# A transformer encoder on one core: the mixers' pieces in another order, with other loads at the start and another final norm

## The chip, the cores and the metric

The kernel runs on one core of one Trainium2 chip. A core has five engines with a program each: TensorE (PE in the profile; PEld is its loading of weights), VectorE (DVE), ScalarE (ACT), GpSimd (POOL) and SyncE (SP), which here only issues DMAs. Each engine works through its own instructions strictly in their order and waits on semaphores of the others. The metric is device time in microseconds of one execution. The kernel before takes 1120.86 us (median of 3 runs, 1120.8 to 1122.6).

## The reference

The input is one sequence of 256 tokens with 1024 channels, all float32. There are two layers, each with two half-weighted feed-forward parts around a mixer:

```python
for l in range(DEPTH):
    x = x + 0.5 * swiglu(rms_norm(x, ln_ffn1[l]), ffn1_w_in[l], ffn1_w_out[l])
    h = rms_norm(x, ln_mix[l])
    x = x + hybrid_mixer(h, w_mix_in[l], conv_w[l], ..., w_mix_out[l], lam_init)
    x = x + 0.5 * swiglu(rms_norm(x, ln_ffn2[l]), ffn2_w_in[l], ffn2_w_out[l])
return rms_norm(x, ln_final)
```

The mixer projects h once and splits it into three kinds of heads, whose outputs are put side by side and projected back:

```python
(wq, wk, wv, dq, dk, dv, dn_qkv, dn_z, dn_beta, dn_a) = jnp.split(h @ w_in, cuts, axis=-1)
o_win = window_attention(wq, wk, wv, sink, slopes)          # 6 query heads on 2 key heads
o_d = diff_attention(dq, dk, dv, lam, slopes)               # 4 heads, difference of two softmaxes
o_diff = rms_norm(o_d, diff_g) * (1.0 - lam_init)
q, k, v = jnp.split(silu(short_conv(dn_qkv, conv_w)), ...)  # 6 heads, width-5 convolution
o_c = gated_delta_chunked(q, k, v, beta, g) + (the same, backwards in time)
o_dn = rms_norm(o_c, dn_g) * silu(dn_z)
return concatenate([o_win, o_diff, o_dn]) @ w_out
```

`gated_delta_chunked` works in 4 chunks of 64 tokens. In each chunk and head, in both directions, it solves a triangular system of 64 (the chunk inverses below, 48 of them), and then a scan carries a 64 x 64 state over the chunks.

## The kernel before, in words

Activations lie transposed in SBUF: `x` is 128 partitions x 8 blocks of channels (`KD`) x 256 tokens.

**Feed-forward.** Weights come from HBM through SP's DMAs in tiles of 128x1024 (512 KB), into 8 raw buffers `wr`. Each is split into two parts of reduced precision: ACT rounds it (`wh`, L264) and DVE takes the residual (`wl`, L265). Each block of 128x256 then takes three matmuls, activation high x weight high, low x high, high x low (`mm3`, L270 to L272). The first two tiles are loaded and split in four parts each (`start`, `ar`, `ah`, `al`, L101 and L102), together with x in four parts, so that the first matmuls can begin early; `prep` scales x by the norm's gain (`xh`, L243, `xl`, L244), and the norm's reciprocal is applied behind the matmuls, so that they needn't wait for it. `sq_add` squares x (L194) and sums (L198); `norm_scale` sums over the channels with a matmul (`fin_ps` and the like, L211), takes a reciprocal root on 128x2 numbers and spreads it (L220).

**Mixer.** It is cut into pieces, and the table `ORDER` is the order in which the program issues them. A scheduler then places the instructions of each piece in each engine's program, and weights are loaded ahead in the order in which the pieces read them. The pieces of which the texts speak:

- `A:n` token projection (`pv`): values and gate inputs. `c:i:b` convolution: a projection (`pj`, L455, 8 matmuls of f32, which the trace counts as 16), taps on ACT and DVE (`pad`, L562, L568). `co` turns conv outputs to tokens (`ptr`), `qn` and `qc` norm q and k and bring them to channels (`kq`, L626).
- `G`, `GS`, `GE`, `GT`: gates, their running sums (`pg`, L507 and L508), exponentials and rows. `E:i` decay exponentials (`XE` from `pe`, L642). `X:p:h` their products with q·k (`pq`, L658).
- `ic`, `i`, `ir:a:b`, `im`, `io`, `ie`: the inverses. `i` transposes XE to `Dg` (L842) and then `L`; `ir` to `io` are a chain of products (`pr`, L825) and sums (`Vi` or `pp`, L826) on DVE, the io's merging blocks of the inverse to larger ones; `ie` transposes `Vi` to `Vc` and `Vt` (L930, L933), multiplies on PE with the gated inputs (`WA`, `W`, `Qc`, L939 to L965).
- `p:n`: projections of attention, 9 to 11 the three groups of local (window) queries, 12 the local keys (`wq`, L683), 13 to 16 the diff heads' queries and keys (`dqk`, L686). `w:b` local scores (L699) and their softmax (L710 to L723), `hw:b` local outputs; `d:h` diff scores (L732, L737, softmax L740 to L753), `h:n` their outputs (`pT`, `PT`, `pso`).
- `sa`, `sb`, `sc`: the scan's steps (`px`, `pS`, `pw`, `pk`, `po`, L995). `z:n` gate projection (`pz`, L466), `ze` its silu (`zt`, L977). `oT` transposes outputs (`pto`), `on` norms the scan's output, `o:part:d` the output projection (`py`).

Some small operations can be given to POOL (with ACT) in place of DVE; `SHARED` lists those that are. `BANK` says for each PSUM tile from which pool it comes: `pm` (2 buffers), `pd` (4), `pt` (2). `lt` loads ACT's table of logarithm and exponential (L202).

**Final norm.** When the last feed-forward has written x, `final` multiplies x with gain and norm in eight operations of 128x256 (`fo`, L1129) and writes it out in four DMAs.

Of the kernel before, what the change touches and what calls it, by code (L numbers as in the profile page):

```python
# [31 lines left out]
NROW = 158  # L32
C_U0, C_U1, C_ONE, C_ID, C_MM = 0, 128, 256, 384, 512
# [23 lines left out]
class Kernel:  # L57
    def __init__(self, ctx, tc, ins, out):
# [12 lines left out]
        self.x = self.xp.tile([P, KD, S], F32, tag="x", name="x")  # L71
        self.col = cp.tile([P, 150], F32, name="col")
# [3 lines left out]
        warm = cp.tile([P, 1], F32, name="warm")  # L76
        nc.scalar.activation(warm, self.onec, AF.Copy)

    def start(self, gcol, pool=None, src=None):

        nc = self.nc
        n = KD // 2
        self.ahead = []
        if pool is not None:
            for j in range(2):
                w, go = self.fetch(src, j * 1024, 1024, n, pool)
                h = pool.tile([P, 1024], F32R, name=f"ah{j}")
                lo = pool.tile([P, 1024], F32R, name=f"al{j}")
                self.ahead.append((w, go, h, lo))
        for i in range(n):  # L90
            nc.sync.dma_start(self.x[:, 2 * i : 2 * i + 2, :], self.ins["x"][:, 2 * i : 2 * i + 2, :])
            for w, go, h, lo in self.ahead:
                go[i]()
            if i == 0:
                nc.scalar.dma_start(self.col, self.ins["cols"])
        for i in range(n):
            for k in (2 * i, 2 * i + 1):
                self.prep(k, gcol, False)
            c = slice(i * 256, i * 256 + 256)
            for w, go, h, lo in self.ahead:  # L100
                nc.scalar.activation(h[:, c], w[:, c], AF.Copy)  # L101
                nc.vector.tensor_tensor(lo[:, c], w[:, c], h[:, c].bitcast(F32), ALU.subtract)  # L102
        self.ahead = [a[2:] for a in self.ahead]
# [99 lines left out]

    def norm_scale(self, name, last=False, log=True):

        nc = self.nc
        ps = self.psum([P, 512], f"{name}_ps", "pt")
        for p in range(2):
            parts = [t for t in (self.sq, self.sq7) if t is not None]
            for t in parts:  # L210
                nc.tensor.matmul(  # L211
                    ps[:, p : p + 1], lhsT=t[:, p * P : (p + 1) * P], rhs=self.onec, start=t is parts[0], stop=t is parts[-1]
                )
        v = self.sp.tile([P, 2], F32, tag="nv", name=f"{name}_v")
# [60 lines left out]
    def ffn(self, l, i, gnext, first, late=False):  # L275
# [3 lines left out]
        with tc.tile_pool(name=f"hp{nm}", bufs=1) as hp, tc.tile_pool(name=f"ht{nm}", bufs=3) as ht:  # L279
# [19 lines left out]
            for j in range(NF):  # L299
# [47 lines left out]
            for d in range(KD):  # L347
# [20 lines left out]
    def mixer(self, l, gnext):  # L368
# [22 lines left out]
        with ExitStack() as ctx:  # L391
# [676 lines left out]
            def out_proj(part, d):  # L1068
# [20 lines left out]
            pieces = {  # L1089
                "clear": clear, "lt": self.log_table, "N": norm, "V": values, "G": gates, "GS": gate_sums, "GE": gate_exps, "GT": gate_rows,  # L1090
# [197 lines left out]
```

## Time and profile before

| | |
|---|---|
| median of 3 runs | 1120.86 us (1120.8 to 1122.6) |
| the profiled execution | 1121.32 us |
| its span, first to last instruction | 1119.5 us |
| mean granted TensorE clock | 0.991 |
| start to the first matmul | 5.86 us |
| first mixer, first `pv` matmul to the output projection's end | 197.6 to about 374 us |
| second mixer | 746.9 to about 924 us |
| last feed-forward matmul begins | 1108.36 us |

The profile is of one execution. The page gives busy times, a chain followed back from the last instruction, and groups of instructions. A timeline lists the instructions in order of time: start, duration, engine, line, operation, output and inputs, form, count, and in brackets how long the engine had been idle and what ended that. Where several alike follow each other they are one row, with a count. The two mixers are alike, so one is read closely.

### The profile page before, as it was taken

What the parts mean: (1) busy time and instruction counts of PE and PEld (TensorE: products, weight loads), DVE (VectorE), ACT (ScalarE), POOL (GpSimd) and SP (SyncE); (2) the same over time, 40 slices, a digit from 0 to 9 for tenths busy, and PEclk for the clock granted to TensorE, in tenths of its full rate; (3) what the DMA queues carried; (4) which work ended last, traced back from release to release, by engine and by line L of the source; (5) the groups of instructions that cost most, each with busy time, mean ns of one, the idle gap of its engine ahead of it and who ended that gap; (6) DMA issues with size and microseconds to landing.
All of it is one profiled execution on the core that took longest, in us unless ns stands there. A gap on an engine that the chain in (4) does not pass through costs nothing.

```text
span 1119.5 us, 22207 instructions
## 1 busy us (share of the span) xinstructions
PE 1077.2 (96%) x9098; PEld 1009.7 (90%) x9098; DVE 751.0 (67%) x1374; ACT 545.4 (49%) x1006; POOL 60.1 (5%) x109
## 2 busy tenths in 40 slices
PE   7999999999799999999999999999989999999996
PEld 7999999777568999999999999988756789999996
DVE  7766654579958866666566666536897697666643
ACT  6544433263773654544444454423648455445441
POOL 0000001100101000000000000121010010000010
PEclk9999999999899999999999999999989999999998
DMA  9655654422322555565555565534223135555521
GB/s 331 225 182 187 199 178 136 132 94 95 113 96 77 165 174 189 182 200 184 171 174 184 188 197 182 170 115 150 85 85 132 42 130 172 189 183 195 187 95 38
DMA packets 49637, 173.65 MB, mean 155 GB/s; under 512 B 5504, under 2 KB 6784, under 8 KB 49536
## 3 DMA queue, kind: packets, MB, share of 16 engines
q1 hardware_dynamic: 49104, 171.64, 46.2%
q8 instruction: 71, 1.16, 0.4%
q10 hardware_dynamic: 432, 0.60, 0.2%
q14 instruction: 30, 0.25, 0.1%
HBM read 171.17 MB, written 1.05 MB: 154 GB/s over the span
## 4 chain that ended last, share of the span: by engine, by line
PE 78%; DVE 13%; ACT 4%; issue 3%; DMA 1%; POOL 1%; DVEq 0%; SPq 0%; ACTq 0%
PE ps L272 21%; PE ps L270 21%; PE ps L271 21%; PE pj L455 4%; PE pv L466 2%; DVE pr L825 2%; DVE wl L265 2%; PE py L270 1%; DVE pp L826 1%; PE py L271 1%; PE py L272 1%; DVE pad L568 1%; ACT wh L264 1%; DVE mxd L740 1%; PE px L995 1%
## 5 line engine op out<-in xcount | busy, mean ns | idle before, releaser
L265 DVE TENSOR_TENSOR wl<-wr,wh 128x1024 fp32r<-128x1024 f32 x270 | 330.5, 1226 | 167.6 <-ACT wh L264 167.1
L264 ACT ACTIVATE wh<-wr 128x1024 fp32r<-128x1024 f32 x270 | 284.2, 1054 | 243.9 <-issue 153.0
L270 PE MATMUL ps<-xh,wh 128*128 128x256 f32 x1336 | 378.6, 283 | 0.6 <-ACT wh L264 0.6
L272 PE MATMUL ps<-xh,wl 128*128 128x256 f32 x1336 | 378.3, 283 | 0.8 <-DVE wl L265 0.8
L271 PE MATMUL ps<-xl,wh 128*128 128x256 f32 x1336 | 377.9, 283 | 0.0
L272 PEld LDWEIGHTS ps<-xh,wl 128*128 128x128 f32 x1336 | 256.3, 192 | 1.2 <-DVE wl L265 1.2
L270 PEld LDWEIGHTS ps<-xh,wh 128*128 128x128 f32 x1336 | 256.3, 192 | 0.8 <-ACT wh L264 0.8
L271 PEld LDWEIGHTS ps<-xl,wh 128*128 128x128 f32 x1336 | 256.3, 192 | 0.0
L270 PE MATMUL ps<-hh,wh 128*128 128x256 f32 x672 | 190.2, 283 | 0.0
L271 PE MATMUL ps<-hl,wh 128*128 128x256 f32 x672 | 190.2, 283 | 0.0
L272 PE MATMUL ps<-hh,wl 128*128 128x256 f32 x672 | 190.2, 283 | 0.0
L455 PE MATMUL pj<-xf,wr 128*128 128x256 f32 x544 | 128.8, 387 | 1.2 <-DVE dqk L686 1.2
L270 PEld LDWEIGHTS ps<-hh,wh 128*128 128x128 f32 x672 | 129.0, 192 | 0.0
L271 PEld LDWEIGHTS ps<-hl,wh 128*128 128x128 f32 x672 | 129.0, 192 | 0.0
L272 PEld LDWEIGHTS ps<-hh,wl 128*128 128x128 f32 x672 | 129.0, 192 | 0.0
L455 PEld LDWEIGHTS pj<-xf,wr 128*128 128x128 f32 x544 | 101.7, 193 | 18.3 <-issue 3.9
L293 ACT ACTIVATE hh<-h 128x256 fp32r<-128x256 f32 x88 | 36.1, 416 | 90.3 <-DVE h L291 90.3
L198 POOL TENSOR_TENSOR sqacc<-sqacc,sqt 128x256 f32<-128x256 f32 x27 | 24.5, 907 | 741.6 <-ACT sqt L194 741.6
L288 DVE TENSOR_TENSOR t<-ps,f_rb 128x256 f32<-128x256 f32 x88 | 36.9, 424 | 38.0 <-PE ps L272 37.7
L294 DVE TENSOR_TENSOR hl<-h,hh 128x256 fp32r<-128x256 f32 x88 | 36.8, 423 | 30.4 <-ACT hh L293 30.4
L194 ACT ACTIVATE sqt<-x 128x256 f32<-128x256 f32 x49 | 19.8, 409 | 56.3 <-DVE x L361 52.5
L568 DVE SCALAR_TENSOR_TENSOR pad<-pad,cwh 128x256 f32<-128x256 f32 x68 | 33.1, 487 | 12.1 <-ACT pad L562 6.8
(319 smaller groups left out, 1212.7 us busy)
## 6 DMA issues: line engine op xcount, KB each, us to landing
wr<-in_ffn SPq DMA_DIRECT2D x258, 512.0 KB, 3.4
wr<-in_mix SPq DMA_DIRECT2D x50, 512.0 KB, 3.4
wr<-in_mix SPq DMA_DIRECT2D x8, 408.0 KB, 3.1
wr<-in_mix SPq DMA_DIRECT2D x8, 384.0 KB, 2.9
x<-in_x SPq DMA_DIRECT2D x4, 256.0 KB, 4.1
ar<-in_ffn SPq DMA_DIRECT2D x8, 128.0 KB, 4.2
cb<-in_constb SPq DMA_DIRECT2D x1, 588.0 KB, 10.2
out_y<-fo SPq DMA_DIRECT2D x2, 256.0 KB, 2.4
```

Of the source, the lines that this page charges most:

```text
L198: (eng or nc.gpsimd).tensor_tensor(self.sq, self.sq, t, ALU.add)
L264: nc.scalar.activation(h, w, AF.Copy)
L265: nc.vector.tensor_tensor(lo, w, h.bitcast(F32), ALU.subtract)
L270: mm(out, lhsT=ah, rhs=bh, start=start, stop=False)
L271: mm(out, lhsT=ah, rhs=bl, start=False, stop=False)
L272: mm(out, lhsT=al, rhs=bh, start=False, stop=stop)
L288: nc.vector.tensor_tensor(t[:rows], gate, rb[:rows], ALU.mult)
L293: nc.scalar.activation(hh[:n, j, :], h[:n], AF.Copy)
L294: nc.vector.tensor_tensor(hl[:n, j, :], h[:n], hh[:n, j, :].bitcast(F32), ALU.subtract)
L455: mm(ps[:, 0:S], lhsT=w[:, k * P : (k + 1) * P], rhs=xf[:, k, :], start=k == 0, stop=k == KD - 1)
L466: mm(st[name][p][:, 0:n], lhsT=xf[:, k, p * P : (p + 1) * P], rhs=w[:, c], start=k == 0, stop=k == KD - 1)
L568: stt(cv, pad[:, w : w + S], cw[:, i * 5 + w : i * 5 + w + 1], cv, ALU.mult, ALU.add)
```

## The change

1. `ORDER` is another order of nearly the same pieces (both layers use it). Behind the token projection the convolution's projections come ahead of the gates; local and diff projections, heads and scores interleave otherwise with the inverses' merges (`io`); the gate projection `z` begins around `ie`, where before it came last in the table; the scan's last step moves behind `on:1`. `BANK` moves the PSUM tiles pq, p1, po, pso and pto from `pd` (4 buffers) to `pt` (2). `SHARED` has 16 entries for 12.
2. At the start x and the table of gains are one DRAM tensor and one tile, loaded by three DMAs from ACT's queue (662, 512 and 1024 columns). The first two weight tiles are packed anew (channel blocks 0 to 3 of both halves in the first, 4 to 7 in the second) and loaded by three DMAs from SP in place of eight. Their split takes four operations of 128x512 on ACT and on DVE for eight of 128x256. Six matmuls on a zero tile are issued ahead of all others.
3. In the final norm ACT multiplies x with the gain (`xg`) while the last feed-forward's outputs are added, three matmuls with no use for their result are issued ahead of the sums and three behind them, and DVE's last multiplication is four operations of 128x512.

```diff
 ORDER = """
...
-io:0 p:9 d:1 p:12 io:1 d:3 w:0 h:2 h:1 p:10 io:2 io:3 io:4 h:3 p:11 w:1 w:2 h:0 hw:0 io:5 ie ce:2 dn hw:1 f g:0 hw:2
...
+io:0 d:3 co:2:2 h:2 p:9 io:1 d:0 w:0 io:2 io:3 h:3 p:10 h:1 p:11 w:1 w:2 io:4 h:0 io:5 hw:0 hw:1 ce:2 ie z:0 dn f z:1
...
 """
-SHARED = set("O2 d0 d1 d2 d3 g5 s3 t1 t8 x4 x5 x6".split())
+SHARED = set("O3 S1 d0 d1 d2 d3 g2 g5 s4 t0 t3 t8 x0 x4 x6 x7".split())
...
     def start(self, gcol, pool=None, src=None):
+            zero = pool.tile([P, S], F32, name="zero")
+            nc.vector.memset(zero, 0.0)
+            wm = self.psum([P, 512], "wm", "pt")
+            for i in range(NWARM):
+                nc.tensor.matmul(wm[:, 0:S], lhsT=zero[:, 0:P], rhs=zero, start=True, stop=True)
             for j in range(2):
-                w, go = self.fetch(src, j * 1024, 1024, n, pool)
+                w, g = self.fetch(src, j * 1024, 1024, 2 - j, pool)
+                go += g
-        for i in range(n):
-            nc.sync.dma_start(self.x[:, 2 * i : 2 * i + 2, :], self.ins["x"][:, 2 * i : 2 * i + 2, :])
-            for w, go, h, lo in self.ahead:
-                go[i]()
-            if i == 0:
-                nc.scalar.dma_start(self.col, self.ins["cols"])
+        cuts = [0] + [NCOL + 512 * i for i in (1, 2, 4)]
+        for a, b in zip(cuts, cuts[1:]):
+            nc.scalar.dma_start(self.xc[:, a:b], self.ins["x"][:, a:b])
...
+    def idle_mm(self, n, tag="pm"):
+        ps = self.psum([P, 512], "idle", tag)
+        for i in range(n):
+            self.nc.tensor.matmul(ps[:, 0:S], lhsT=self.ident, rhs=self.cst[:, C_U0 : C_U0 + S], start=True, stop=True)
...
                 if gnext is None:
                     self.sq_add(d, last=d == KD - 1)
+                    if d == 0:
+                        self.xg = self.xp.tile([P, KD, S], F32, tag="xh", name="xg")
+                    nc.scalar.activation(self.xg[:, d, :], self.x[:, d, :], AF.Copy, scale=self.col[:, 48 + d : 49 + d])
...
     def final(self, name):
-        for k in range(KD):
-            nc.vector.scalar_tensor_tensor(o[:, k, :], self.x[:, k, :], self.col[:, 48 + k : 49 + k], rb, ALU.mult, ALU.mult)
+        for i in range(KD // 2):
+            k = slice(2 * i, 2 * i + 2)
+            nc.vector.tensor_tensor(o[:, k, :], self.xg[:, k, :], rb.unsqueeze(1).to_broadcast([P, 2, S]), ALU.mult)
```

Three places in the first mixer show what the new table does to the engines' programs. Lines of the changed kernel have moved by 12 to 27.

On PE, behind the token projection (`pv`), the kernel before goes through five blocks of conv projections and then the gate sums (`pg`):

```order
L466 MATMUL pv<-wr,xf 128x408 x2
L455 MATMUL pj<-xf,wr 128x256 x40
L507 MATMUL pg<-bgs,cst 128x12 x2
L508 MATMUL pg<-bgs,cst 128x24
L436 MATMUL ptr<-cst,cs 128x128 x2
```

The changed kernel has there:

```order
L493 MATMUL pv<-wr,xf 128x408 x2
L482 MATMUL pj<-xf,wr 128x256 x40
L463 MATMUL ptr<-cst,cs 128x128 x4
L482 MATMUL pj<-xf,wr 128x256 x8
L463 MATMUL ptr<-cst,cs 128x128 x4
L482 MATMUL pj<-xf,wr 128x256 x8
L534 MATMUL pg<-bgs,cst 128x12 x2
L535 MATMUL pg<-bgs,cst 128x24
```

Two more blocks of projections and two groups of transposes now stand ahead of the gate sums.

On DVE, around the inverses' first merges, the kernel before has this ahead of the first local scores (`wq` comes first for the queries p:9, then for the keys p:12; `pr` is a product and `Vi` or `pp` a sum of the inverses, `mxd`, `smd` and `c` belong to the diff heads' softmax):

```order
L683 SCALAR_TENSOR_TENSOR wq<-pj,m_rb 128x256
L825 TENSOR_TENSOR pr<-L,Vi 128x1024
L747 RECIPROCAL c_3108<-smd 128x2
L740 TENSOR_REDUCE mxd<-pss 128x2
L748 SCALAR_TENSOR_TENSOR c_3108<-smd,nlam,c_3108 128x2
L740 TENSOR_REDUCE mxd<-pss 128x2
L749 RECIPROCAL smd<-smd 128x2
L826 TENSOR_REDUCE pp<-pr 128x16x8
L825 TENSOR_TENSOR pr<-Vi,pp 128x1024
L265 TENSOR_TENSOR wl<-wr,wh 128x1024
L747 RECIPROCAL c_3163<-smd 128x2
L683 SCALAR_TENSOR_TENSOR wq<-pj,m_rb 128x256
```

The changed kernel has this there (`wq` is now that of the keys):

```order
L710 SCALAR_TENSOR_TENSOR wq<-pj,m_rb 128x256
L853 TENSOR_REDUCE pp<-pr 128x8x8
L774 RECIPROCAL c_3112<-smd 128x2
L767 TENSOR_REDUCE mxd<-pss 128x2
L775 SCALAR_TENSOR_TENSOR c_3112<-smd,nlam,c_3112 128x2
L767 TENSOR_REDUCE mxd<-pss 128x2
L776 RECIPROCAL smd<-smd 128x2
L852 TENSOR_TENSOR pr<-L,Vi 128x1024
L853 TENSOR_REDUCE pp<-pr 128x16x8
L774 RECIPROCAL c_3151<-smd 128x2
L852 TENSOR_TENSOR pr<-Vi,pp 128x1024
L775 SCALAR_TENSOR_TENSOR c_3151<-smd,nlam,c_3151 128x2
```

The keys' `wq` has moved ahead by a merge's products; that of the queries comes next behind the last row, behind the product `pr` and with no weight residual (`wl`) between.

On PE the first local scores (`pss` from `wq`) stand so in the kernel before:

```order
L737 MATMUL pss<-dqk 128x256 x4
L699 MATMUL pss<-wq 128x256 x4
L455 MATMUL pj<-xf,wr 128x256 x4
L436 MATMUL pT<-cst,sc 128x128 x4
L455 MATMUL pj<-xf,wr 128x256 x4
```

In the changed kernel the first local scores have this ahead of them:

```order
L463 MATMUL pT<-cst,sc 128x128 x4
L482 MATMUL pj<-xf,wr 128x256 x8
L811 MATMUL pso<-V,PT 128x64 x4
L759 LDWEIGHTS sdiag
L759 MATMUL pss<-ddb,sdiag 128x512
L759 LDWEIGHTS sdiag
L759 MATMUL pss<-ddb,sdiag 128x512
L764 MATMUL pss<-dqk 128x256 x4
L726 MATMUL pss<-wq 128x256 x4
```

A diff head's output and another one's scores now stand ahead of them.

On ACT, at the inverses' end, the kernel before has (`W` and `WA` are copies of the inverses, `zt` the silu of the gate projection, `p` the products with them, `oh` attention outputs):

```order
L942 COPY W<-Vt 32x12x32 x2
L791 ACTIVATE hn<-O 128x512
L765 ACTIVATE PT<-pT 128x512 x2
L977 ACTIVATE zt<-pz,rth 128x384 x2
L775 ACTIVATE oh<-pso 128x256
L202 ACT_TABLE_LOAD
L956 ACTIVATE Qc<-p_3494 128x384
L765 ACTIVATE PT<-pT 128x512
L965 COPY W<-p_3544 32x12x32
L765 ACTIVATE PT<-pT 128x512
L965 COPY W<-p_3592 32x12x32
L775 ACTIVATE oh<-pso 128x256
```

The changed kernel has there:

```order
L969 COPY W<-Vt 32x12x32 x2
L802 ACTIVATE oh<-pso 128x256
L818 ACTIVATE hn<-O 128x512
L792 ACTIVATE PT<-pT 128x512
L983 ACTIVATE Qc<-p_3501 128x384
L792 ACTIVATE PT<-pT 128x512
L1004 ACTIVATE zt<-pz,rth 128x384
L992 COPY W<-p_3561 32x12x32
L992 COPY W<-p_3588 32x12x32
L1004 ACTIVATE zt<-pz,rth 128x384
L214 ACT_TABLE_LOAD
L1045 ACTIVATE SC<-px 128x384
```

Both `zt` and the table load have moved from ahead of `Qc` to behind it.

More of the change, by code (lines that the diff above doesn't have):

```diff
@@ L32 @@
 NROW = 158
+NCOL = 150
+NWARM = 6
 C_U0, C_U1, C_ONE, C_ID, C_MM = 0, 128, 256, 384, 512
@@ L47 @@
 BANK = dict(
-    pj="pm", pv="pd", pz="pm", py="pm", pss="pd", pg="pt", pgr="pd", ptr="pd", pkq="pt", pe="pd", pq="pd", p1="pd",
-    p2="pt", pk="pd", px="pt", pS="pt", po="pd", pw="pt", pT="pd", pso="pd", pto="pd",
+    pj="pm", pv="pd", pz="pm", py="pm", pss="pd", pg="pt", pgr="pd", ptr="pd", pkq="pt", pe="pd", pq="pt", p1="pt",
+    p2="pt", pk="pd", px="pt", pS="pt", po="pt", pw="pt", pT="pd", pso="pt", pto="pt",
 )
-SHARED = set("O2 d0 d1 d2 d3 g5 s3 t1 t8 x4 x5 x6".split())
+SHARED = set("O3 S1 d0 d1 d2 d3 g2 g5 s4 t0 t3 t8 x0 x4 x6 x7".split())
 C_M0, C_M1, C_DD, C_WD, C_SEL = 0, 64, 128, 640, 1152
@@ L70, in __init__ @@
         cp = self.cp
-        self.x = self.xp.tile([P, KD, S], F32, tag="x", name="x")
-        self.col = cp.tile([P, 150], F32, name="col")
+        self.xc = self.xp.tile([P, NCOL + KD * S], F32, tag="x", name="x")
+        self.col = self.xc[:, 0:NCOL]
+        self.x = self.xc[:, NCOL:].rearrange("p (k t) -> p k t", k=KD)
         self.cst = None
@@ L75, in __init__ @@
         nc.vector.memset(self.onec, 1.0)
-        warm = cp.tile([P, 1], F32, name="warm")
-        nc.scalar.activation(warm, self.onec, AF.Copy)
     def start(self, gcol, pool=None, src=None):
         nc = self.nc
+        self.ahead = []
         n = KD // 2
-        self.ahead = []
+        go = []
         if pool is not None:
+            zero = pool.tile([P, S], F32, name="zero")
[3 more added lines that the diff above has]
+                nc.tensor.matmul(wm[:, 0:S], lhsT=zero[:, 0:P], rhs=zero, start=True, stop=True)
             for j in range(2):
-                w, go = self.fetch(src, j * 1024, 1024, n, pool)
+                w, g = self.fetch(src, j * 1024, 1024, 2 - j, pool)
+                go += g
                 h = pool.tile([P, 1024], F32R, name=f"ah{j}")
                 lo = pool.tile([P, 1024], F32R, name=f"al{j}")
-                self.ahead.append((w, go, h, lo))
-        for i in range(n):
-            nc.sync.dma_start(self.x[:, 2 * i : 2 * i + 2, :], self.ins["x"][:, 2 * i : 2 * i + 2, :])
-            for w, go, h, lo in self.ahead:
-                go[i]()
-            if i == 0:
-                nc.scalar.dma_start(self.col, self.ins["cols"])
+                self.ahead.append((w, h, lo))
+        cuts = [0] + [NCOL + 512 * i for i in (1, 2, 4)]
+        for a, b in zip(cuts, cuts[1:]):
+            nc.scalar.dma_start(self.xc[:, a:b], self.ins["x"][:, a:b])
+        warm = self.cp.tile([P, 1], F32, name="warm")
+        nc.scalar.activation(warm, self.onec, AF.Copy)
+        for g in go:
+            g()
         for i in range(n):
@@ L98, in start @@
                 self.prep(k, gcol, False)
-            c = slice(i * 256, i * 256 + 256)
-            for w, go, h, lo in self.ahead:
+            if self.ahead:
+                w, h, lo = self.ahead[i // 2]
+                c = slice(i % 2 * 512, i % 2 * 512 + 512)
                 nc.scalar.activation(h[:, c], w[:, c], AF.Copy)
                 nc.vector.tensor_tensor(lo[:, c], w[:, c], h[:, c].bitcast(F32), ALU.subtract)
-        self.ahead = [a[2:] for a in self.ahead]
+        self.ahead = [a[1:] for a in self.ahead]
     def constants(self):
@@ L213, in norm_scale @@
                 )
+        if last:
+            self.idle_mm(3)
         v = self.sp.tile([P, 2], F32, tag="nv", name=f"{name}_v")
```

28 lines of the change are left out of this document (17 added, 11 removed).

## The prediction

> **What bounds the kernel now.** I read the page first, for the shares and the chain that ended last.
>
> ```profile
> span 1119.5 us, 22207 instructions
> PE 1077.2 (96%) x9098; PEld 1009.7 (90%) x9098; DVE 751.0 (67%) x1374; ACT 545.4 (49%) x1006; POOL 60.1 (5%) x109
> PE 78%; DVE 13%; ACT 4%; issue 3%; DMA 1%; POOL 1%; DVEq 0%; SPq 0%; ACTq 0%
> ```
>
> PE is busy for 1077.2 of 1119.5 us, so 42.3 us are all that any order can win on it. The chain leaves PE for 22% of the span, and mostly for DVE. That share is an average, so next comes the view by windows: the stretch, its length, then busy time and number of instructions of PE, PEld, DVE, ACT and POOL, the granted clock, the DMA share, GB/s.
>
> ```profile
> 14.00:197.00 183.00, 181.57 (x1508) 181.04 (x1509) 115.37 (x180) 83.78 (x116) 5.78 (x6) 1.00 0.59 200
> 230.00:250.00 20.00, 18.84 (x150) 15.04 (x148) 15.33 (x49) 17.27 (x58) 1.14 (x7) 1.00 0.24 79
> 250.00:285.00 35.00, 29.85 (x151) 23.04 (x148) 34.48 (x66) 14.12 (x38) 3.27 (x3) 0.98 0.29 91
> 285.00:300.00 15.00, 12.60 (x64) 10.15 (x64) 13.98 (x22) 9.00 (x22) 3.55 (x2) 0.82 0.45 141
> 300.00:315.00 15.00, 13.81 (x76) 8.89 (x75) 12.61 (x31) 14.82 (x46) 0.00 (x0) 1.00 0.32 114
> 330.00:345.00 15.00, 14.61 (x319) 13.28 (x314) 10.65 (x20) 4.14 (x9) 1.02 (x1) 1.00 0.01 2
> 345.00:360.00 15.00, 14.03 (x204) 13.14 (x201) 14.00 (x30) 6.43 (x14) 2.41 (x10) 1.00 0.33 106
> 835.00:850.00 15.00, 13.71 (x70) 10.99 (x70) 13.69 (x20) 9.79 (x25) 3.55 (x2) 0.84 0.41 141
> ```
>
> The feed-forward stages (first row) leave PE 1.4 us of idle in 183; the change does not touch their middle. What can move is in the two mixers, of which the rows show the first (197 to about 374) and, last, the slow place of the second (747 to about 924), which looks the same. Each mixer has three limits in turn. From 250 to 300 it is DVE, busy for 48.46 of 50 us, with the inverses of the chunk matrices. From 300 to 315 it is ACT, with the softmaxes. After 330 it is PE. The largest hole on PE lies under the DVE part, and the timeline there shows why (start, length, engine, line, operation, in brackets idle time and what ended it):
>
> ```profile
> 281.88 2.66 DVE L825 TENSOR_TENSOR pr<-Vi,pp 128x1024 f32<-128x1024 f32 x1
> 284.45 1.22 DVE L265 TENSOR_TENSOR wl<-wr,wh 128x1024 fp32r<-128x1024 f32 x1
> 285.66 0.41 DVE L683 SCALAR_TENSOR_TENSOR wq<-pj,m_rb 128x256 f32<-128x256 f32 x1
> 286.21 2.17 PE L699 MATMUL pss<-wq 64*128 64x256 f32 x8 [5.77 <-DVE c L748]
> 288.31 2.97 PE L455 MATMUL pj<-xf,wr 128*128 128x256 f32 x8
> ```
>
> PE stands for 5.77 us. The profile names c, the last small DVE operation; the one that PE needs is wq, the local key, which started behind a 2.66 us product and a weight residual. Afterwards eight projection matmuls cost 2.97 us, where the 80 of a row further down cost 17.43, or 1.74 for eight; the granted clock of that window is 0.82. So the hole costs PE 5.77 us and then some 15 x 0.18 = 2.7 us of clock, 12.6/15 of it in busy time: 2.3. **8.1 us per mixer** is what stands there to be had.
>
> **The change, part by part.**
>
> *Local projections earlier.* In the new order the keys' projection (p:12) comes a merge and more ahead of the local scores, and head 0's diff scores with the matmuls of head 2's output stand between. The wq that PE waited for is done well before; what PE waits for now is wq of the first query group, behind another such product on DVE, but with other work in front of it (16 projection matmuls of the trace's count at 0.22, 3.5 us, transposes, diff scores). I take the 5.77 us as gone from PE. It does not follow that the mixer is 5.77 us shorter: DVE is busy in 48.46 of 50 us there, and its work is not less. It issues the same products, reductions, residuals and scalings; one slope operation moves to PE, and one more piece (the late conv piece c:2:2, with its sums) comes in from before. I count +0.6 to +0.8 us of DVE work between the start of the inverses and their end. What DVE can win is its idle time there, 1.5 us. So the end of the inverses, Vc, moves by the sum of that and of its start.
>
> *Gate sums later.* This is the part that could hurt.
>
> ```profile
> 209.53 17.43 PE L455 MATMUL pj<-xf,wr 128*128 128x256 f32 x80
> 226.79 0.51 PE L507 MATMUL pg<-bgs,cst 128*128 128x12 f32 x4
> 231.09 0.69 PE L436 MATMUL ptr<-cst,cs 128*128 128x128 f32 x4
> 236.42 1.38 ACT L642 ACTIVATE XE<-pe,ngc 128x64 f32<-128x64 f32 x6
> 245.30 2.66 ACT L626 COPY kq<-pkq 64x192 f32<-64x192 f32 x8
> 247.37 1.02 DVE L658 TENSOR_TENSOR XE<-XE,pq 128x384 f32<-128x384 f32 x2 [0.27 <-PE pq L649]
> 251.82 3.39 DVE L842 STREAM_TRANSPOSE Dg<-XE 32x384 f32<-32x384 f32 x4
> ```
>
> Before the gate sums PE runs 40 projection matmuls (80 in the trace's count, each f32 matmul being two). Now 56, and eight transposes: 16 x 17.43/40 = 7.0 us more, and 8 x 0.69/4 = 1.4, less some overlap. The gate sums come some 8 us later, and the decay exponentials that hang on them: 12 of the 24 now follow the key and query copies on ACT, 12 x 1.38/6 = 2.8 us, where the last copy ended at 247.9. Their products with pq were the last thing before Dg at 251.8. In turn the conv work and its scalings have gone ahead, and ACT and DVE had 2.7 and 4.7 us idle in the window from 230 to 250, so most of the 8 us is taken up. I take Dg 2 us later (0 to 8), less 0.6 for conv scalings no longer between products and transposes; against 1.5 us of DVE idle partly recovered this makes **Vc later by 0.7 us** (from -2 to +8, both ends kept for the range).
>
> *The end of the inverses.* Here ACT is the limit.
>
> ```profile
> 302.58 1.23 DVE L930 STREAM_TRANSPOSE Vc<-Vi 128x1024 f32<-128x1024 f32 x1
> 322.03 1.05 ACT L977 ACTIVATE zt<-pz,rth 128x384 f32<-128x384 f32 x2
> 323.71 1.28 ACT L202 ACT_TABLE_LOAD   x1
> 325.00 0.49 ACT L956 ACTIVATE Qc<-p 128x384 f32<-128x384 f32 x1
> 329.51 0.92 PE L995 MATMUL px<-vtok,W 64*64 64x64 f32 x24
> ```
>
> Between Vc and Qc ACT is busy nearly throughout. The change puts zt (1.05) and the table load (1.28) behind Qc, 2.3 us; with the softmax operations that run earlier or later than before I count 2.7 us less for ACT there: Qc 2.7 us earlier relative to Vc. Behind Qc the two W copies now follow each other, with one PT between instead of a PT each and an oh, so px comes about 1 us sooner after Qc. The table load then stands ahead of the copy of px, and takes back some 0.8. px: +0.7 - 2.7 - 1.0 + 0.8 = -2.2. From there PE is the limit (14.61 of 15 us), and the new order leaves it 1.8 us more behind px (a pso of 1.4 and transposes of 0.4) that before stood ahead; they can fill the hole that PE has from 345 to 360 (15 - 14.03 = 0.97 us), so I charge little. **-2.0 us per mixer**, from +6 to -8.
>
> *POOL.* The list of shared operations has 16 entries for 12. The products of 128x1024 that ran beside a POOL sum of scores took 1.91 and (above) 2.66 us, where the residual of the same size took 1.22, so a POOL operation can cost DVE its own length:
>
> ```profile
> 287.34 1.26 POOL L753 TENSOR_TENSOR sc<-sc 128x512 f32<-128x512 f32 x1 [4.56 <-DVE Vi L826]
> 288.49 1.91 DVE L825 TENSOR_TENSOR pr<-Vi,pp 128x1024 f32<-128x1024 f32 x1
> ```
>
> The Trainium skill, SBUF — State Buffer, section "SBUF: two separate sides", says that a DVE operation with two SBUF inputs and a GpSimd operation reading SBUF exclude each other for the whole instruction; by that the overlap costs the full length of POOL's operation, and the trace agrees as to the order of size: 2.66 is 1.44 over 1.22, beside a POOL operation of some 1.26, while 1.91 is 0.7 over. The new POOL operations lie in the conv and scan stretches, where DVE has room; the four score sums stay. I charge nothing, at most 1 us a mixer, and the cover is DVE's idle time there.
>
> *Start.* The loads become three and three instead of twelve and one, x goes over ACT's queue, and the split of the first weights has four operations of 512 columns on each engine for eight of 256.
>
> ```profile
> 5.86 0.58 PE L270 MATMUL ps<-xh,ah 128*128 128x256 f32 x1 [5.86 <-ACT ah L101]
> 9.99 0.41 PE L270 MATMUL ps<-xh,ah 128*128 128x256 f32 x1
> 10.55 0.28 PE L270 MATMUL pu<-xh,ah 128*128 128x256 f32 x1
> 15.87 0.39 PE L272 MATMUL ps<-xh,wl 128*128 128x256 f32 x1 [0.76 <-DVE wl L265]
> 18.13 1.06 ACT L264 ACTIVATE wh<-wr 128x1024 fp32r<-128x1024 f32 x1 [2.32 <-DMA wr<-in_ffn]
> 27.48 1.22 DVE L265 TENSOR_TENSOR wl<-wr,wh 128x1024 fp32r<-128x1024 f32 x1
> ```
>
> SP issued 12 loads at about 0.45 us each, so the first streamed tile was issued at 6.86. With three issues ahead it goes out some 4 us sooner, and 2.32 us of ACT's wait at 18.13 go. But DVE is the limit up to the residual at 27.48: its work is the same less four overheads, so it wins what it stood idle behind that wait, 2.3 us, less a little because the first matmul now needs half a tile of weights for 128 columns. **-2.1 us**, from -0.5 to -3. The six warm-up matmuls on zeros touch no data. PE ran cold from 5.86 to about 10.3 us (a matmul of 0.41 at 9.99, of 0.28 at 10.55). If they end that before the data come, PE saves 4.4 x (1 - 1.74/2.97) = 1.8 us, which DVE does not let it keep: nothing more, at most 1.8. The Trainium skill, TensorE: Matmul & The Clock Gate, Part 1, says that some 3.4 us of steady work lift the throttle and an idle window as long restores it. By that the warm-up, 6 x 2 x 2.97/8 = 4.5 us, would suffice if data come within 3.4 us of its end; the trace's 4.4 us of cold running agrees roughly.
>
> *Final norm.* The gain is applied beforehand on ACT, beside the last feed-forward's output.
>
> ```profile
> 1110.13 0.38 PE L211 MATMUL fin_ps<-onec,sqt 128*128 128x1 f32 x2 [1.37 <-ACT sqt L194]
> 1113.02 3.22 DVE L1129 SCALAR_TENSOR_TENSOR fo<-x,col,fin_pb 128x256 f32<-128x256 f32 x8 [0.81 <-PE fin_pb L220]
> 306.42 0.67 DVE L710 SCALAR_TENSOR_TENSOR sc<-wd,pss 128x512 f32<-128x512 bf16 x1
> ```
>
> Four operations of 128x512, by the last row, whose 0.67 includes some 0.07 of overlap with the next, 4 x 0.6 = 2.4, for 3.22: -0.8. Three idle matmuls, 6 x 0.22 = 1.3 us, about fill the 1.37 us in which PE waits for the last square; they can hold the sums back by a part of it, say 0.25. **-0.6 us**, from -1 to +0.3. The gained copy of the last piece, 0.4 on ACT, lies behind that piece's square, beside PE's sums; if it came first it would cost its 0.4.
>
> **Sum:** -2.1 - 2 x 2.0 - 0.6 = -6.7 on 1121.32, the profiled execution's time (its span of 1119.5 and 1.8 around it): 1114.6. That execution is 0.46 over the median of 1120.86, inside the spread of the three runs; I forecast **1114.5**.
>
> **Rivals.**
>
> *PE gets all of its hole back:* 8.1 us in each mixer, if DVE's order, not its work, was the limit. For it: PE is 96% of the span, and DVE's work has 1.5 us of slack only as long as nothing of it leaves the stretch. Against it: 48.46 of 50 us on DVE. 1121.3 - 16.2 - 2.7 = 1102.4.
>
> *No gain in the mixers:* DVE-bound to Vc, and what ACT gains after it is used up by PE's work moved behind px. 1121.3 - 2.7 = 1118.6, or 1118.1 against the median. For it: each stage has its own limit, and PE has 14.61 of 15 us after 330.
>
> *Slower, by the gates:* if the 8 us of the later gate sums go through to Dg and Vc, px is 8 - 2.9 = 5.1 us later, in both mixers +10.2, with start and tail -2.7: 1128.8. It decides from a delay of Vc of 2.9 + 1.35 = 4.3 us on. For it: the chain of sums, rows, exponentials, products and transposes has no way around; at 247.37 the products wait for pq only 0.27 us. Against it: ACT's and DVE's idle time from 230 to 250, 7.4 us together.
>
> *The reorder does not do what it says:* PE's hole simply moves, for pj behind the inverses' first operation, or for wq of the query group behind the product of 2.66 us. That is the case without gain, and I price it with it.
>
> **How the numbers follow.** Forecast 0.58, PE's whole hole 0.10, no gain 0.17, slower by the gates 0.15 (of which a third in part only, near no change). The likeliest case's own range is 1111 to 1118.5. The range is 1105 to 1123: below lies most of the first rival, above two thirds of the last one. What a measurement can tell from no change is 0.2%, 2.2 us: under 1118.6 is faster. Faster: 0.53 + 0.10 + 0.10 = 0.73; same: 0.05 + 0.07 + 0.04 = 0.16; slower 0.11.
>
> **What would show it.** Right: no wait over 2 us on PE in the mixer, and the clock at 1.00 through it; DVE still busy for over 95% between Dg and Vc, and Vc less than 2 us from before, counted from the mixer's start; Qc some 2 us earlier; the residual that ended at 28.7 some 2 us earlier; fo in 2.4 us. Wrong: Dg more than 4 us later (the gates), or Vc earlier by over 4 (the first rival); a table load that delays the copy of px by its 1.28; a first matmul later than 8 us without a warm clock.

## The result: slower, and the profile after

| | before | changed |
|---|---|---|
| median | 1121.62 us (1120.8 to 1122.6, 4 runs) | 1128.20 us (1126.9 to 1130.24, 4 runs) |
| ratio | | 1.0057, 95% interval 1.0045 to 1.007 |
| span of the profiled execution | 1119.5 us | 1126.4 us |

The median of the kernel before is of one run more than the three above. One execution of a kernel below (with two idle matmuls) took 1313.67 us at a mean granted clock of 0.75, and the figures leave it out.

The page of the changed kernel (engines' busy times, then the chain) does not look slower at first sight: PE's share went up, DVE's busy time fell.

```profile
PE 1091.4 (97%) x9122; PEld 1016.5 (90%) x9124; DVE 742.2 (66%) x1357; ACT 550.1 (49%) x1014; POOL 70.3 (6%) x117
PE 79%; DVE 12%; ACT 5%; issue 2%; DMA 1%; POOL 0%; DVEq 0%; ACTq 0%
```

The view of PE's waits over the whole kernel shows the hole at the local scores gone: 11.3 us for both mixers before, 0.5 now. Other waits have taken its place (us in all, times, longest; the first fence is of before).

```profile
PE pss L699 <- DVE c L748: 11.3, 2, 5.8
PE pso L784 <- ACT PT L765: 2.4, 2, 1.2
PE pT L436 <- POOL sc L753: 2.4, 2, 1.2
```

```profile
PE pj L482 <- DVE dqk L713: 4.6, 2, 2.3
PE pso L811 <- ACT PT L792: 3.2, 4, 1.0
PE pT L463 <- ACT sc L770: 2.4, 2, 1.2
PE pss L759 <- ACT sc L770: 2.2, 2, 1.1
PE pss L726 <- DVE wq L710: 0.5, 2, 0.3
```

So I cut the first mixer at its own events and asked for the windows between them: the start of the token projection, the first gate sum, the first Dg, Vc, the first px (with which the scan begins), the px of its second, third and fourth step, the first matmul of the last transposes of O, and a moment shortly behind the end. Before, from `Dg` on, with the sum of all nine windows:

```profile
251.80:302.60 50.80, 43.24 (x222) 33.71 (x222) 48.70 (x89) 25.25 (x70) 6.82 (x5) 0.93 0.33 104
302.60:329.51 26.91, 25.10 (x302) 16.01 (x298) 17.11 (x50) 24.40 (x61) 0.00 (x0) 1.00 0.36 120
329.51:335.42 5.91, 5.65 (x133) 5.12 (x132) 4.32 (x9) 2.59 (x6) 0.00 (x0) 1.00 0.00 0
335.42:341.12 5.70, 5.57 (x131) 5.01 (x132) 3.96 (x8) 0.49 (x1) 0.00 (x0) 1.00 0.01 3
341.12:349.37 8.25, 8.25 (x151) 7.58 (x151) 6.44 (x13) 2.55 (x6) 1.02 (x1) 1.00 0.21 68
349.37:358.96 9.59, 8.62 (x103) 8.15 (x103) 8.90 (x20) 4.75 (x9) 2.41 (x10) 1.00 0.32 101
358.96:375.00 16.04, 15.11 (x123) 14.64 (x123) 14.34 (x28) 10.71 (x21) 0.75 (x1) 1.00 0.42 137
sum 177.43, PE 164.62 PEld 131.79 DVE 140.17 ACT 97.85 POOL 18.47; mean PE 18.29 PEld 14.64 DVE 15.57 ACT 10.87 POOL 2.05
```

The changed kernel:

```profile
253.00:304.90 51.90, 45.46 (x227) 34.20 (x226) 49.10 (x93) 26.78 (x76) 8.00 (x5) 0.97 0.34 110
304.90:328.46 23.56, 21.76 (x276) 13.54 (x277) 13.93 (x41) 21.23 (x54) 0.00 (x0) 1.00 0.27 91
328.46:337.55 9.09, 8.94 (x133) 7.29 (x132) 5.15 (x13) 4.93 (x10) 1.65 (x2) 1.00 0.19 59
337.55:344.39 6.84, 6.84 (x142) 6.23 (x142) 5.10 (x9) 1.54 (x3) 0.64 (x1) 1.00 0.25 81
344.39:352.49 8.10, 8.10 (x152) 7.49 (x151) 6.57 (x13) 2.63 (x5) 0.00 (x0) 1.00 0.22 67
352.49:362.15 9.66, 8.26 (x119) 7.79 (x118) 8.63 (x19) 4.75 (x11) 3.47 (x11) 1.00 0.25 75
362.15:378.00 15.85, 14.84 (x105) 14.18 (x106) 12.90 (x26) 9.53 (x20) 1.41 (x1) 0.89 0.37 123
sum 181.35, PE 168.72 PEld 133.39 DVE 135.89 ACT 98.65 POOL 23.53; mean PE 18.75 PEld 14.82 DVE 15.10 ACT 10.96 POOL 2.61
```

PE's idle time in the mixer is what it was: 177.43 - 164.62 = 12.8 us before, 181.35 - 168.72 = 12.6 now. In the last five windows, from px on, it is 2.3 us before and 2.6 now. The stage from Vc to px has become 3.4 us shorter (2.9 forecast). Then the first step of the scan takes 9.1 us in place of 5.9, the second 6.8 in place of 5.7. In the last window the granted clock is 0.89, since a spell of half clock lies in it, a stretch in which the granted clock is 0.50. Counted from the mixer's first matmul, by the starts in the timeline (us; "last pto" is the last matmul of the last transposes of O, "end" the last one of the output projection; the second mixer agrees within 0.1):

| | pg | Dg | Vc | px | last pto | end |
|---|---|---|---|---|---|---|
| before | 29.2 | 54.3 | 105.0 | 131.9 | 162.2 | 174.1 |
| changed | 37.0 | 56.3 | 108.2 | 131.7 | 166.0 | 177.9 |

### The profile page after: what moved, and what is told of

Read it like the earlier page. It is cut to its first block, busy times and chain, and to the rows that moved or that the text cites. A ratio compares the mean times of both kernels' runs of the same rounds, so it can differ in the third digit from the quotient of the medians.

```text
span 1126.4 us, 22219 instructions
## 1 busy us (share of the span) xinstructions
PE 1091.4 (97%) x9122; PEld 1016.5 (90%) x9124; DVE 742.2 (66%) x1357; ACT 550.1 (49%) x1014; POOL 70.3 (6%) x117
## 4 chain that ended last, share of the span: by engine, by line
PE 79%; DVE 12%; ACT 5%; issue 2%; DMA 1%; POOL 0%; DVEq 0%; ACTq 0%
PE ps L294 21%; PE ps L292 21%; PE ps L293 21%; PE pj L482 5%; DVE pr L852 2%; PE pv L493 2%; DVE wl L287 1%; PE py L292 1%; PE py L293 1%; PE py L294 1%; DVE Vi L853 1%; DMA wr<-in_ffn 1%; ACT kq L653 1%; PE pss L764 1%; DVE Dg L869 1%
## 5 line engine op out<-in xcount | busy, mean ns | idle before, releaser
L293 PEld LDWEIGHTS ps<-xl,wh 128*128 128x128 f32 x1336 | 252.4, 189 | 0.0
L294 PEld LDWEIGHTS ps<-xh,wl 128*128 128x128 f32 x1336 | 251.9, 189 | 0.5 <-DVE wl L287 0.4
L292 PEld LDWEIGHTS ps<-xh,wh 128*128 128x128 f32 x1336 | 250.6, 188 | 0.1
L292 PEld LDWEIGHTS ps<-hh,wh 128*128 128x128 f32 x672 | 126.2, 188 | 0.0
L294 PEld LDWEIGHTS ps<-hh,wl 128*128 128x128 f32 x672 | 125.8, 187 | 0.0
L292 PE MATMUL py<-oh,wh 128*128 128x256 f32 x128 | 38.6, 307 | 2.7 <-DVE x L1109 2.0
## 6 DMA issues: line engine op xcount, KB each, us to landing
cb<-in_constb SPq DMA_DIRECT2D x1, 588.0 KB, 11.2
```

Source lines behind the costliest of these rows:

```text
L292: mm(out, lhsT=ah, rhs=bh, start=start, stop=False)
L293: mm(out, lhsT=ah, rhs=bl, start=False, stop=False)
L294: mm(out, lhsT=al, rhs=bh, start=False, stop=stop)
```

## The experiments

Each was timed beside the kernel before on the same chip (its median there 1121.6 to 1122.3 us); the ratios are to it.

**The parts of the change.** The first kernel (x1) keeps the changed start and final norm and takes the three tables of before:

```diff
-ORDER, BANK, SHARED of the change
+ORDER, BANK, SHARED of before
```

> The changed start and final norm with the three tables (ORDER, BANK, SHARED) of before. Theory one, read off the two traces: the start brings the mixer forward by 0.84 us, the final norm brings nothing, and all of the loss of 6.6 us comes out of the mixers: 1121.6 - 0.8 = 1120.8. Rival, the prediction's two steps: start -2.1 and final norm -0.6, 1118.9.

Measured: 1120.98 us, ratio 0.9985 (0.9975 to 0.9995). Start and norm together win about 1.7 us, between the two theories; so the mixers lose about 8.

The next one (x4) has, of the tables, ORDER of the change alone:

```diff
-BANK, SHARED of the change
+BANK, SHARED of before
```

> The changed kernel with BANK and SHARED of before, so that of the three tables only ORDER is new. Theory one, the order of the pieces makes the loss: 1128.2 within 1.5. Rival, the loss is made by the PSUM tiles that moved to a pool of two buffers (pso, pto, p, po wait for a free one) and by POOL's work: most of the 6.6 us come back, 1123.

1123.24 us, ratio 1.0011 (1.0002 to 1.0021). The rival was right, and the theory that the order makes the whole loss fell. Against the kernel with all three tables of before (0.9985) the order still costs 0.0026. Two kernels (x5 with BANK of before, whose edit is shown, and x6 with SHARED of before) take the tables apart:

```diff
-    ... pq="pt", p1="pt", ... po="pt", ... pso="pt", pto="pt",
+    ... pq="pd", p1="pd", ... po="pd", ... pso="pd", pto="pd",
```

> The changed kernel with BANK alone of before (pq, p1, po, pso and pto from the pool of four buffers). With BANK and SHARED of before the time fell by about 5 us. Theory one, the pool of two buffers makes it, since the attention outputs, the scan's products and the transposes of O now wait for each other: ratio to before 1.001 to 1.002, as with both. Rival, SHARED makes it: the ratio stays at 1.005 or more.

> The changed kernel with SHARED alone of before (other operations on POOL, the slopes of the third local head on DVE again). Theory one (the pool of two buffers): nothing of the 5 us comes back, ratio 1.005 to 1.006. Rival (POOL's work and its collisions with DVE, or the third head's scores without a slope operation): ratio 1.001 to 1.002.

With BANK of before alone: 1121.93 us, ratio **0.9998** (0.9989 to 1.0008). With SHARED of before alone: 1127.17, 1.0044 (1.0029 to 1.0059). **The move of five PSUM tiles from a pool of four buffers to one of two is worth as much as the whole loss against the kernel before**, 0.0059 of the ratio, 6.6 us. That holds beside the new SHARED; beside the old one the move costs 0.0033 (1.0044 for 1.0011), so the tables don't act each for itself.

What it does to the program is seen at the scan's first step. In the changed kernel (timeline, start and duration first):

```profile
329.57 0.91 PE L1022 MATMUL px<-vtok,W 64*64 64x64 f32 x22
331.74 0.91 PE L1022 MATMUL pS<-SC,raw 64*64 64x64 f32 x24
332.58 1.08 PE L801 MATMUL pso<-PT,V 128*64 128x256 f32 x8
333.60 0.66 PE L463 MATMUL pto<-cst,O 128*128 128x128 f32 x4
334.18 0.62 PE L1022 MATMUL pk<-SC,kq 64*64 64x64 f32 x13
337.55 0.92 PE L1022 MATMUL px<-SC,W 64*64 64x64 f32 x24
```

With BANK of before, and everything else as changed:

```profile
329.04 0.91 PE L1022 MATMUL px<-vtok,W 64*64 64x64 f32 x22
329.87 1.08 PE L801 MATMUL pso<-PT,V 128*64 128x256 f32 x6
330.88 0.66 PE L463 MATMUL pto<-cst,O 128*128 128x128 f32 x4
331.71 0.92 PE L1022 MATMUL pS<-SC,raw 64*64 64x64 f32 x24
333.21 0.92 PE L1022 MATMUL pk<-SC,kq 64*64 64x64 f32 x24
335.57 0.91 PE L1022 MATMUL px<-SC,W 64*64 64x64 f32 x24
```

In the pool of four, pso and pto run in the gap between px and pS, in which PE waits for the copy of px anyway. In the pool of two they come after pS, ahead of pk: px, pS, pw and now po, pso and pto are given the same two buffers in turn. A step of the scan is a chain (px, its copy, pS, its copy, pk, two sums, the next px), and there they stand in it; whether that is what the move costs, the next runs had to tell. From the first px to the last transposes the way is 34.3 us in the changed kernel and 31.6 with BANK of before.

Do two or three of the tiles make it? Four kernels put some back:

```diff
-    po="pt", pso="pt", pto="pt", pq="pt", p1="pt"
+    (x9)  pso="pd", pto="pd"
+    (x10) po="pd"
+    (x13) pso="pd", pto="pd", po="pd"
+    (x14) pq="pd", p1="pd"
```

> The changed kernel with pso and pto alone from the pool of four buffers, as before. BANK as a whole was worth 6.6 us. Theory one (in the pool of two, the last output and the transposes must take their turn between the scan's tiles, and stand in the scan's chain between pS and pk): the first step of the scan, px to the next px, falls from 9.1 to about 7.6 us, and this is half of what BANK costs: ratio 1.002 to 1.003. Rival (po in the pool of two makes it): the first step stays at 9.1 us, ratio 1.005 to 1.006.

> The changed kernel with po alone from the pool of four buffers, as before. Theory one: the first step of the scan stays at 9.1 us, the second falls from 6.84 to 5.8 us, since pk no longer stands behind po and pw in their turn; some 1 us in each mixer: ratio 1.004. Rival (po makes all of it): first step 7.6 us, ratio 1.000 to 1.001.

> The changed kernel with pso, pto and po from the pool of four buffers, and pq and p1 still from the pool of two. Alone, pso with pto brought 0.0008 and po 0.002 of the 0.0059 that BANK costs. Theory one (the scan's tiles and the outputs block each other, and each one alone leaves the other in the way): together they bring nearly all, the way from the first px to the last pto falls from 34.3 to about 31.7 us, ratio 0.999 to 1.001. Rival (the rest is in pq and p1): ratio 1.003.

> The changed kernel with pq and p1 alone from the pool of four buffers. Theory one (the scan's tiles make it): Dg, Vc and Qc stay within 0.3 us, ratio 1.005 to 1.006. Rival (the products of key and query and the inverses' ends wait for the two buffers): Dg or Qc come 1 to 2 us earlier, ratio 1.002 to 1.003.

Ratios 1.0049, 1.0037, 1.0038 and 1.0031 (each within 0.0015). Each brings 0.001 to 0.003, none all, and my theory of the parts fell in its numbers. With pso and pto put back the first step still takes 9.2 us. With po put back the second takes 7.2 and not 5.8. With all three the way from the first px to the last pto is 34.8 us and not 31.7. With pq and p1 alone Dg comes 0.2 us earlier and Qc 0.6, less than the rival said, at nearly its ratio. In the first of these kernels most of pso runs ahead of px, but ACT's queue has been planned anew with it, and now the table load stands in the same chain, between pS and its copy:

```profile
331.76 0.92 PE L1022 MATMUL pS<-SC,raw 64*64 64x64 f32 x24
331.83 0.57 ACT L1004 ACTIVATE zt<-pz,rth 128x384 f32<-128x384 f32 x1
332.43 1.28 ACT L214 ACT_TABLE_LOAD   x1
333.72 0.49 ACT L1055 ACTIVATE SC<-pS 128x384 f32<-128x384 f32 x1
334.73 0.92 PE L1022 MATMUL pk<-SC,kq 64*64 64x64 f32 x24
```

In the kernel with all five back the table load runs at 329.74, beside px. That the parts don't add up is shown; which planning decision each of them turns was not followed further.

How much the scan can explain is seen on the whole way from the first px to the end, in mixers with no spell of half clock on it:

| tables of the change | kernel | first px to end, us |
|---|---|---|
| none | before | 42.1 |
| ORDER | x4 | 45.1 |
| ORDER and BANK | x6 | 45.1 |
| ORDER and SHARED | x5 | 43.5 |
| all three | x3, x8 (below) | 45.2 |

The order alone makes this way 2.9 us longer. BANK adds 1.7 us beside the new SHARED and nothing beside the old. A mixer without a spell takes 175.3 us with all three tables (x3) and 173.2 with BANK of before (x5). So in two mixers some 4.3 of the 6.6 us are BANK's without the clock. The rest goes with spells of half clock: four fell into the mixers of the changed kernel's profiled execution and one into those of x5, and the mean clock was 0.991 to 0.993 in the runs of the one and 0.993 to 0.997 in those of the other.

**Where pso and pto are issued.** To move them by hand instead (x2):

```diff
-ie z:0 dn f z:1 g:1 g:0 sa:0 sb:0 hw:2 oT:3:4 sc:0
+ie z:0 dn f z:1 g:1 g:0 hw:2 oT:3:4 sa:0 sb:0 sc:0
```

> The changed kernel, with the last local output and the transposes of O (pso 1.08 us and pto 0.66 us on PE) ahead of the scan's first step again, as in the kernel before. Theory one, the chain of the scan sets the end of the mixer up to the last transposes, and these two stand in it between pS and pk: the four steps of the scan get 1.7 us shorter in each mixer, 1128.2 - 3.4 = 1124.8. Rival, PE is the limit there and has the same work wherever it stands: 1128.2 within 0.5.

1132.66 us, ratio 1.0091: worse by 4. The first step did fall, from 9.1 to 6.0 us, but px came at 135.4 in place of 131.7, since it now waited behind the output and the transposes, and the half clock lasted 10.2 us in each mixer in place of 6.8. The theory was right as to the step, and wrong as to the sum.

**The half clock.** In the changed kernel PE runs at half rate for 3.4 us behind the last transposes:

```profile
362.00:364.00 2.00, 1.49 (x9) 1.08 (x10) 1.90 (x4) 1.34 (x5) 1.41 (x1) 1.00 0.51 199
364.00:366.00 2.00, 2.00 (x11) 1.98 (x12) 0.68 (x2) 0.31 (x1) 0.00 (x0) 0.60 0.77 225
366.00:368.00 2.00, 2.00 (x12) 2.00 (x12) 1.00 (x3) 0.94 (x3) 0.00 (x0) 0.55 0.10 41
368.00:370.00 2.00, 2.00 (x19) 2.00 (x19) 1.51 (x4) 2.00 (x5) 0.00 (x0) 1.00 0.00 0
```

Two microseconds hold 11 or 12 matmuls there in place of 19. To see whether PE's short wait ahead of them (1.06 us) brings it, two idle matmuls were put into that wait (`wm`, x3):

```diff
-o:0:7 o:1:0
+o:0:7 wm wm o:1:0
```

> The changed kernel with two idle matmuls (0.44 us each) on PE right ahead of the last transposes of O, in the 1.06 us in which PE waits there. Theory one, the half clock for 3.41 us behind these transposes comes of the idle time ahead of them: the spell at 364.4 us is gone in both mixers, and 1.7 us each with it, 1128.2 - 3.4 = 1124.8. Rival, the spell has another cause (the small matmuls, or a limit on power): it stays or moves, 1128.2 and up to 0.5 more in each mixer for the idle matmuls.

1124.57 us, ratio 1.0022 (1.0011 to 1.0033): 0.0035 or 3.9 us less, near theory one's 3.4. In its profiled execution the clock was 1.00 in both mixers, although the program up to the idle matmuls near the first mixer's end is that of the changed kernel, in which another spell stood at 275.6 to 279.1 us. So whether that one comes differs from execution to execution. That the wait brings the later spell is not shown: the profiled executions of x6, x8, x9, x13 and x14 have a wait of 1.0 to 1.3 us at that place, without idle matmuls, and no spell behind it. The times of the kernel with idle matmuls lie in groups: 1122.9 to 1123.0 at a mean clock of 0.998, 1124.4 to 1124.6 at 0.996 to 0.997, 1126.0 to 1126.2 at 0.995: steps of some 1.6 us, one spell each.

**The hole at the local scores by itself.** The kernel before, with one piece moved (x7):

```diff
-io:0 p:9 d:1 p:12 io:1 d:3 w:0
+p:12 io:0 p:9 d:1 io:1 d:3 w:0
```

> The kernel before with one piece moved: the local keys' projection p:12 ahead of the merge io:0, so that the local scores find their keys. Theory one (DVE is the limit from Dg to Vc): the wait of 5.77 us on PE goes or shrinks, Vc stays within 1 us, and the time within 2 us of before, less up to 1.7 us in each mixer if the half clock behind the wait goes: ratio 0.997 to 1.001. Rival (PE gets its hole back): 8 us in each mixer, ratio 0.986.

1139.03 us, ratio 1.0145: neither. Vc came at 104.1, 0.9 us earlier, as theory one says. The hole stayed at 5.12 us, now with another end, and holes of 2.1 and 3.3 us came behind it; the scan began at 140 of the mixer's time in place of 132, and the half clock lasted 24 us in the first mixer. What it cost is shown; why ACT ended the inverses 6.5 us later (Qc at 133.9 for 127.4) is open.

```profile
286.92 2.98 PE L699 MATMUL pss<-wq 64*128 64x256 f32 x8 [5.12 <-ACT sc L743]
312.47 1.10 PE L784 MATMUL pso<-V,PT 128*128 128x64 f32 x8 [2.09 <-ACT PT L765]
326.67 0.65 PE L774 MATMUL pso<-PT,V 128*64 128x256 f32 x2 [3.32 <-ACT PT L765]
```

**The gates' sums, and a faster version.** The changed kernel with the sums (`GS`) moved ahead (x8):

```diff
-V c:0:0 c:1:0 c:1:1 c:1:2 G c:0:2 co:1:0 ... c:2:1 GS ce:1
+V c:0:0 c:1:0 c:1:1 c:1:2 G GS c:0:2 co:1:0 ... c:2:1 ce:1
```

> The changed kernel with the gates' sums directly behind the gates, so that they stand behind 32 projection matmuls where the changed kernel has 56. Theory one, the later sums make Dg 2.1 us later and that passes through to the end of the mixer: Dg and Vc 2 us earlier, 4 us less in all, ratio 1.002. Rival, Dg is set by the order of the conv pieces and the products and not by the sums: Dg stays, ratio 1.0057 within 0.001.

1123.73 us, ratio 1.0031 (1.0009 to 1.0053). pg came 11.2 us earlier and Dg only 0.9; the runs go from 1121.1 us at a mean clock of 0.998 to 1130.8 at 0.990, so that most of this difference is the clock's, and neither theory is decided. With BANK of before as well, without (x11) and with (x12) the two idle matmuls, and without them with SHARED of before (x15):

> The changed kernel with BANK of before and with the gates' sums directly behind the gates. With BANK of before alone the ratio was 0.9998, and with the early sums alone Dg came 0.9 us earlier. Theory one (both act in their own place): 1 us less in each mixer, ratio 0.998. Rival (Vc does not follow Dg): ratio 1.000, and more where the half clock falls at another place.

> The same with two idle matmuls ahead of the last transposes of O. Theory one (they keep the clock where a spell of half clock would begin, and cost nothing where none does): equal to the run without them or up to 1.7 us less in each mixer, ratio 0.996 to 0.998. Rival (they hold the transposes back): up to 0.5 us more in each mixer.

> The fastest kernel so far (BANK of before, early sums of the gates; ratio 0.9959) with SHARED of before as well. Theory one (SHARED is worth little by itself, 0.0013 at most alone): 0.995 to 0.997. Rival (POOL's larger share of the work is what lets the new order win): 0.998 or more.

1117.80 us, ratio **0.9959** (0.9946 to 0.9973); 1119.24, 0.9971; 1120.75, 0.9986 (0.9977 to 0.9995). The first **beats both kernels**, by the ratios the one before by 4.6 us (0.0041) and the changed one by 11 (0.0098). The idle matmuls win nothing where no spell stands behind the transposes; they make the way from px to the end 0.35 us longer. The rival to the last kernel was right: the new SHARED is worth 0.0027 here, and the way from px to the end is 45.1 us without it and 43.5 with it. Beside the changed BANK that way is the same with either (45.1 and 45.2).

## Why the prediction was wrong

It said 1114.5 us and a range of 1105 to 1123; it was 1128.2.

- **Local projections earlier.** Right: the wait at the local scores went, and the mixer did not get shorter by it. DVE stayed busy for 49.1 of 51.9 us from Dg to Vc. PE's idle time came back in pieces.
- **Gate sums later.** Right for Dg: 2.0 us later forecast, 2.1 measured. Vc was to be 0.7 us later and came 3.2 later. In the execution without spells (the two idle matmuls; the same program up to there) it was at 106.55, 1.5 us later; so 1.6 of the 2.5 us of that miss are a spell of half clock.
- **The end of the inverses.** From Vc to px, -2.9 us forecast, -3.4 measured. px was to be 2.2 us earlier and was 0.2 earlier, and 1.8 in the execution without spells. Up to px, the sum held but for the clock.
- **Behind px: the step that failed.** "From there PE is the limit (14.61 of 15 us), and the new order leaves it 1.8 us more behind px ... they can fill the hole that PE has from 345 to 360 ... so I charge little." From px to the end the mixer took 42.1 us before and takes 46.2, +4.0. The moved work filled no hole: PE's idle time on this way went from 2.3 us to 2.6, its busy time from 40.1 to 43.9. A spell of half clock behind the last transposes makes 1.0 of the +4.0. Of the other 3.0 the order makes 2.9 by itself (x4), and 1.4 stay when BANK alone is put back (x5). So the work moved behind px had to be charged in full, and more: 1.7 us of pso and pto now stand in the scan's first step, and the same 192 matmuls of the output projection keep PE busy for 28.4 us there in place of 26.3 (27.3 without the spell). How the 3.0 us divide between the scan's chain and PE's own work is not shown. BANK is in no term of my sum: I described it and gave it no price.
- **The clock, the other step.** "The clock at 1.00 through it" was to show the forecast right, and the sum had no term for spells of half clock. Taking away one long wait did not end them. Before, one spell of 6.8 us in each mixer began 3.1 us into the hole, and its first 2.7 us met no work; now two of 3.4 in each mixer fall on work throughout. By the execution without spells they cost 2.6 us a mixer (177.9 for 175.3), 1.6 ahead of Vc and 1.0 behind the last transposes.
- **The sum of a mixer.** -2.0 us forecast, +3.8 measured. Of the miss of 5.8 us, 2.8 lie behind px without the clock, 2.6 are the spells, and 0.4 lie ahead of px.
- **Start.** -2.1 forecast; the first mixer began 0.84 us earlier. The residual that started at 27.48 came at 25.84, 1.6 us earlier for some 2 forecast. But DVE was not the limit up to there: ACT's rounding of that tile waited for PE, 1.75 us before and 1.26 now. What the start won is idle time of PE: from 14 to 40 us it stood for 1.4 us before and for 0.65 now. The waits for the first streamed tiles went. In their place PE waits 0.4 us for the squares' sums, which now stand behind the residuals on DVE, and 0.2 for a residual. The first norm came 1.6 us later, and no wait of PE shows behind it (the first two rows are of before, the others of the change):

```profile
24.88 1.06 ACT L264 ACTIVATE wh<-wr 128x1024 fp32r<-128x1024 f32 x1 [1.75 <-PE ps L271]
28.62 0.42 DVE L226 COPY f_rb<-f_pb 128x256 f32<-128x256 f32 x1
```

```profile
22.62 1.06 ACT L286 ACTIVATE wh<-wr 128x1024 fp32r<-128x1024 f32 x1 [1.26 <-PE ps L293]
22.96 0.60 PE L231 MATMUL f_ps<-onec,sqacc 128*128 128x1 f32 x4 [0.38 <-DVE sqacc L210]
25.84 1.22 DVE L287 TENSOR_TENSOR wl<-wr,wh 128x1024 fp32r<-128x1024 f32 x1
30.18 0.42 DVE L248 COPY f_rb<-f_pb 128x256 f32<-128x256 f32 x1 [0.82 <-PE f_pb L242]
```

- **Final norm.** -0.6 forecast, +0.2 measured. The last multiplication took 2.48 us for 3.22, as forecast, and the sums came 0.2 us later behind the idle matmuls. So far it held. But the four writes, now issued closer together, landed in 2.5 to 3.0 us for 2.4 to 2.5: from the end of fo to the end of the span 4.1 us for 3.3, which had no term.
- **The rivals.** "Slower, by the gates" was near in its number (1128.8) and wrong in its mechanism: the gates moved Dg by 2.1 us, not by 8. "No gain" let PE's work behind px use up what ACT gained, and it lost 4.0 us there against a gain of 3.4. No rival named the scan's chain, the PSUM pools or the clock.

## What to carry over

Work that is moved into a stage where an engine is nearly always busy is free only if that engine's idle time there shrinks by it. Here it was to fill a hole, and the idle time behind px stayed (2.3 and 2.6 us). So price moved work in full, unless the trace shows the wait that it fills. A table that moves tiles between PSUM pools adds no instruction, and here it was worth 6.6 us through the order; price it by what then shares a buffer in turn, and try it beside the other tables, since their effects don't add up. Taking one engine's longest wait away gained nothing here while another engine was busy throughout, so compare the idle time's sum and not its largest item. And compare executions with as many spells of half clock, or count the spells first.

## What the runs showed of the hardware

The granted clock falls to one half in spells of 3.41 us or a multiple (6.83, 13.65). In the mixers one of 3.41 was worth 1.6 us ahead of Vc and 1.0 behind the last transposes. In each profiled execution the spells begin whole multiples of 3.413 us apart, as in the changed kernel: 88.75 us, or 26 of them, from the first spell to the second, and 552.96, or 162, to the third. Here a spell came after a wait of only 1.06 us with transposes behind it, and one after a stretch in which PE waited for 1.08 us and then ran the diff heads' scores (matmuls of 32 rows among them); before, it began 3.1 us into a wait of 5.77 us. After waits of 1.0 to 1.3 us at the first of these places five other kernels showed none. Whether it comes at the same place differs between executions of one program, so single runs differ by some 1.6 us and its multiples: ten runs of one kernel (x8) lie between 1121.1 us at a mean clock of 0.998 and 1130.8 at 0.990.

The Trainium skill, TensorE: Matmul & The Clock Gate, Part 1, gives a window of about 3.4 us, and calls it free-running; the spells' length here, and that they come and go between executions, agree with that. Its advice in the section on HAM oscillation, no idle gap of PE above some 3.4 us, would not have kept these spells away: the 1.06 us lie far below it. That page's second failure mode, many short idles between groups of matmuls, is nearer to what stands here; no run tests it.
